# Where the high weight tiles and the w2k buffers of a two-layer mixer kernel start in SBUF

## The chip, the cores and the metric

The kernel runs on one core of a Trainium2 chip. The metric is the device time of one execution in microseconds (us). A measurement of this kernel before the change is three executions, of which the median counts; one further execution was profiled.

## The reference

Two layers of a mixer, on 256 latent and 256 context tokens of width 2048. Each layer normalises and modulates its input, multiplies it by one wide matrix, and gives the columns to three branches, whose outputs go through an output matrix. Cut to what matters here:

```python
for l in range(DEPTH):                     # 2 layers
    h = rmsnorm(x, g_pre[l]) * (1.0 + scale[:, None]) + shift[:, None]
    h_c = rmsnorm(ctx, g_pre[l]) * (1.0 + scale_c) + shift_c
    proj, proj_c = h @ w_in[l], h_c @ w_in[l]          # (256, 2048) @ (2048, 5120)
    k_ctx, v_ctx = heads(pc[4], 2), heads(pc[5], 2)    # of proj_c
    y = mixer_branches(proj, latent_attn, ...)         # gMLP, windowed attention, Fourier
    x_new = x + gate[:, None] * rmsnorm(y @ w_out[l], g_post[l])
    if not last:                                       # the context stream, in layer 0 alone
        y_c = mixer_branches(proj_c, ctx_attn, ...)
        ctx = ctx + gate_c * rmsnorm(y_c @ w_out[l], g_post[l])
    x = x_new
```

All inputs and the output are float32. In the last layer the context is needed for keys and values only.

## The kernel before

**Split operands.** TensorE multiplies in the type float32r, which keeps fewer bits than float32. So each operand is split into a high part (a cast on ScalarE) and a low part (the rest, a subtraction on VectorE), and a product is made of three matmuls: high by high, high by low, low by high. `mm3` (L576 to L578) issues them. Weights are stationary (they are loaded with LDWEIGHTS), activations are the moving operand, 512 columns wide in layer 0 (256 latent and 256 context tokens).

**Layer 1's units.** In layer 1 only the latent tokens are needed for most columns. There `hh[k]` holds the high part of the activations in its first 256 columns and the low part in the other 256, and `mm2` (L732, L733) makes the same three products with two matmuls: the high weights against all 512 columns, and the low weights against the first 256. I call the two a pair. `tunit1` runs a unit (128 output columns) as 16 pairs, one for each of 16 tiles of the inner dimension; the two units for the keys run the pairs for latent and context both. The phases of layer 1, in order, are named au, cx, ag, cg, k, v, q, bg.

```python
    def mm2(ps, w, h, k):
        PE.matmul(ps, w[0], h, start=k == 0, stop=False)
        PE.matmul(ps[:, 0:S], w[1], h[:, 0:S], start=False, stop=k == KT - 1)
```

**The stream of weights.** `Stream` (object `W`) holds all weight tiles of 128 x 1024 in the order of their use: layer 0's units, layer 0's output matrix, layer 1's units, layer 1's output matrix. Each is loaded by a DMA from SyncE's queue into one of three `raw` buffers, and `emitting` (L544, L546) casts it into a `whi` tile on ScalarE and writes the rest into a `wlo` tile on VectorE. `twins` (L554) does the same for the value weights in another arrangement. `whi` and `wlo` are rings of four buffers each. The stream runs three tiles ahead of its use (`AHEAD`). Some tiles have places of their own (`place`). A unit takes two tiles, eight of the sixteen inner tiles from each, 512 bytes of each partition for one LDWEIGHTS.

**The ring's order.** The 214 high tiles that go through the ring take the four buffers in turn, except that the tiles numbered 5, 8, 11, 14, 113, 116, 119 and 122 (from 0) take the buffer that is second in turn, since its last reader comes first there.

**Other work on the engines.** The attention, Fourier and gating branches are generators that `Later` steps between the matmuls of the units, by an estimate of the time that has passed. Their temporaries are the seven `w2k` buffers of 512 floats: queries as stationary operand, probabilities and transposed probabilities (L593, L594, L1176) as moving operand, and so on. Next to it, VectorE forms the modulation of the next layer from streamed weights (`mods`). TensorE's order is the order of the source; VectorE's, ScalarE's and SyncE's follow priorities after layer 0's first stage.

**Where tiles stand.** `HOMES` (L93) lists the tiles with long-lived places; they are allocated one behind the other, from byte 16,512 of each partition on, in steps of 32 bytes. Because the sizes ahead of them add up so, `w2k` (from 51,712), `wlo`, the activations `hh` and `hl`, and all four `whi` buffers (94,720, 98,816, 102,912, 107,008) start at multiples of 512 bytes. The small tiles (`es`, `mx`, `nm`, `den`, `rs_a`, the modulation vectors) stand behind the homes.

Of the kernel before, what the change touches and what calls it, by code (L numbers as in the profile page):

```python
# [7 lines left out]
F32 = mybir.dt.float32  # L8
F32R = mybir.dt.float32r
# [4 lines left out]
P = 128  # L14
D = 2048
KT = D // P
S = 256
# [49 lines left out]
def trunk_kernel(ctx: ExitStack, tc: tile.TileContext, xT, xhalf, cT, wss, wsl, wmod, win, wout0, wout1, const, vec, rows,  # L67
                 wmat, bs, sink, out):
    nc = tc.nc
    V, A, G, PE, DMA = nc.vector, nc.scalar, nc.gpsimd, nc.tensor, nc.sync  # L70
# [3 lines left out]
    W2K = 7  # L74
    cnt = [0]

    def sb(shape, dt, tag, bufs=1):
        cnt[0] += 1
        return pool.tile(shape, dt, tag=tag, bufs=bufs, name=f"{tag}_{cnt[0]}")

    def w2k(shape, dt=F32):
        return sb(shape, dt, "w2k", W2K)
# [5 lines left out]
    def ms_ps(name="ms"):  # L88
        cnt[0] += 1
        return psum.tile([P, 512], F32, tag="ms", bufs=2, name=f"ps_{name}_{cnt[0]}")  # L90


    HOMES = ([("ct", 32, 1), ("cs", 32, 1), ("gs0", 32, 1)] + [(f"yy{i}", 1024, 1) for i in range(8)]  # L93
             + [("join", 256, 2), ("w2k", 512, W2K), ("mraw", 1024, 2)]
             + [(tag, 1024, n) for tag, n in (("macc", 1), ("vv", 1), ("raw", 3), ("whi", 4), ("wlo", 4), ("mg", 1), ("mgl", 1))]
             + [(f"{tag}{i}", 512, 1) for i in range(KT) for tag in ("hh", "hl")]
             + [(tag, 512, 1) for tag in ("acc", "ctrh", "ctrl", "nstrh", "nstrl", "ws", "bsb", "kt1")]
             + [("identr", P, 1), ("ones", P, 1), ("red", P, 2), ("m0r", P, 1), ("rbs", S, 2), ("kt0", 2 + KT * 32, 1)])
    for tag, n, bufs in HOMES:
        sb([P, n], F32, tag, bufs)  # L100

# [9 lines left out]
    ct = sb([P, KT, 2], F32, "ct")  # L111
    vecs = sb([P, 2, NVEC], F32, "vecs")
    cst = sb([P, NKEEP - P], F32, "cst")
    ones = sb([P, P], F32, "ones")
    V.memset(ones, 1.0)
    mhalf8 = sb([P, 8], F32, "mhalf")
    mhalf = mhalf8[:, 0:4]
# [19 lines left out]
    class low:  # L137


        def __init__(self, n):  # L140
            self.n = n
# [16 lines left out]
    identr = sb([P, P], F32R, "identr")  # L158
# [5 lines left out]
    gg0 = sb([P, KT, 2], F32, "gg0")  # L164
# [223 lines left out]
    state = {"ctx": [], "phase": "", "owed": 0.0}  # L388
# [43 lines left out]
    class Later:  # L432
# [19 lines left out]
        def flush(self):  # L452
# [6 lines left out]

    OUT = list(range(8, KT)) + list(range(8))  # L460
    NHI, NLO, NRAW = 4, 4, 3
    TAIL = [(("hl0 hl1", 1), ("hl2 hl3", 1)), (("hl4 hl5", 1), ("hl6 hl7", 1)),
            (("mraw", 2), ("mraw", 2)), (("macc", 1), ("ws bsb", 1)),
            (("yy4", 1), ("yy5", 1)), (("yy6", 1), ("yy7", 1))]
# [6 lines left out]
    class Stream:  # L471
        AHEAD = 3

        def __init__(self):
            self.src, self.out, self.pos, self.stop = [], [], 0, 0
            self.raws, self.rest = [], []
            self.place, self.behind, self.twin = {}, {}, set()
            for l in range(2):
                def half(name, i, h):
                    return win[l, UIDX[name][i], h]  # L480
                for i in range(2):
                    a = [half("av", 2 * i, 0), half("au01", i, 0), half("av", 2 * i, 1),
                         half("av", 2 * i + 1, 0), half("au01", i, 1), half("av", 2 * i + 1, 1)]
                    if l == 0:
                        a.insert(3 - i, half("au2", 0, i))
                        self.place[len(self.src) + 3 - i] = AU2[i]
                    self.src += a
                for i, u in enumerate(UNITS):
                    if u[0] not in ("av", "au01") + ("au2",) * (l == 0):
                        if u[0] == "v":  # L490
                            self.twin.update((len(self.src), len(self.src) + 1))
                        self.src += [win[l, i, 0], win[l, i, 1]]
                if l == 0:
                    self.src += [wout0[j, i] for j in OUT for i in range(2)]
                else:
                    self.src += [wout1[c, i] for c in range(4) for i in range(8)]
                if l == 0:
                    n = len(self.src) - 2 * HELD
                    self.place[n] = (("mraw", 2), ("mraw", 2))
                    self.place[n + 1] = (("macc", 1), ("mg", 1))  # L500
            for i, tags in enumerate(TAIL):
                self.place[len(self.src) - len(TAIL) + i] = tags
            self.raw_place = {len(self.src) - len(TAILRAW) + i: tags for i, tags in enumerate(TAILRAW)}
# [16 lines left out]
        def load_rest(self):  # L520
            n, r = self.rest.pop(0)
            DMA.dma_start(r[:, 512:], self.src[n][:, 512:])

        def emitting(self, cut=1024):

            if len(self.raws) == len(self.out):
                self.load()
            n = len(self.out)
            r = self.raws[n]
            if n in self.twin:  # L530
                yield from self.twins(r)
                return
            tags = self.place.get(n, (("whi", NHI), ("wlo", NLO)))
            hi, lo = ([sb([P, 1024 // len(t[0].split())], F32R, tag, t[1]) for tag in t[0].split()] for t in tags)
            self.out.append((hi, lo))
            cut = min(cut, 1024 // max(len(hi), len(lo), len(r) if isinstance(r, list) else 1))
            for i in range(0, 1024, cut):
                c = slice(i, i + cut)
                ph, pl = part((hi, lo), c)
                rc, _ = part((r, r), c)  # L540
                with ExitStack() as after:
                    for i in self.behind.get(n, ()):
                        after.enter_context(tc.issue_after(i.ins))
                    A.copy(ph, rc)  # L544
                yield
                self.last = V.tensor_tensor(out=pl, in0=rc, in1=ph.bitcast(F32), op=ALU.subtract)  # L546
                yield

        def twins(self, r):

            self.out.append([sb([P, 2, 2, 256], F32R, tag, n) for tag, n in (("whi", NHI), ("wlo", NLO))])
            for i, t in enumerate(self.out[-1]):
                rc = r[:, i * 512:(i + 1) * 512].rearrange("p (k c) -> p k c", c=256)
                A.copy(t[:, :, 0], rc)  # L554
                yield
                self.last = V.tensor_tensor(out=t[:, :, 1], in0=rc, in1=t[:, :, 0].bitcast(F32), op=ALU.subtract)
                yield
# [22 lines left out]
    def part(w, c):  # L580

        def of(t):
            if not isinstance(t, list):
                return t[:, c]
            n = t[0].shape[-1]
            return t[c.start // n][:, c.start % n:c.start % n + c.stop - c.start]

        return of(w[0]), of(w[1])
# [724 lines left out]
    def finish():  # L1313
# [16 lines left out]
        later.add(turn(), YT)  # L1330
        state["phase"] = "out1"
        state["ones"] = sb([P, P], F32R, "join", 2)
        A.copy(state["ones"], ones)
        sums = sb([P, 2, 4], F32, "sums")
        gy = {}
        tot = sb([P, 2], F32, "tot")
# [65 lines left out]
    rbs = {}  # L1402
# [89 lines left out]
    with tc.manual_schedule(engines={EN.PE}):  # L1492
# [5 lines left out]
        raw = w2k([P, NFIRST])  # L1498
# [5 lines left out]
        for i in range(KT):  # L1504
# [12 lines left out]
            for a in range(2):  # L1517
                k = 2 * j + a
# [14 lines left out]
        for h, ps in enumerate((ms_ps("rs"), mm_ps("rs"))):  # L1533
            for j in range(2):
                c = slice(h * S + j * P, h * S + (j + 1) * P)
# [31 lines left out]
        state["acc"] = out_proj()  # L1567
        layer(1)
        finish()


# [75 lines left out]
```

## Time and profile before

| | |
|---|---|
| median of three executions | 1119.2 us (1117.8 to 1120.15) |
| the profiled execution | 1119.12 us |
| its span, first to last instruction | 1117.3 us |
| TensorE matmuls, busy | 1107.5 us (99%) |
| weight loads (PEld), busy | 927.7 us (83%) |
| VectorE, busy | 926.3 us (83%) |
| ScalarE, busy | 550.4 us (49%) |
| granted TensorE clock | 1.00 |

A page of the profile gives the busy time of each engine and groups of instructions; the longer answers of the trace list groups of a stretch of time (source line, engine, operation, output and input tiles, shape and type, count, then busy us, mean ns of one, and the idle time ahead of them with what ended it), or single instructions in the order of time (start in us from the span's start, duration in us, engine, line, operation). Busy time of matmuls says little: they are pipelined, each takes longer than the distance to the next, and their ends are modelled. The distance from one start to the next is what a matmul costs.

Roughly, layer 0's first stage lasts until 128 us, its units until 495 us, its output matrix until about 718 us; layer 1's first stage lasts from 729 to 763 us, its units until 1016.6 us, and its output matrix until the end.

### The profile page before, as it was taken

To read this page: it belongs to the slowest core of one execution; us is meant where nothing else is said; L and a number is where in the kernel's file an instruction comes from. 1 tells how busy PE (TensorE), PEld (TensorE's weight loads), DVE (VectorE), ACT (ScalarE), POOL (GpSimd) and SP (SyncE) were. 2 spreads that over 40 slices of the span, in tenths; PEclk is the share of its full clock that TensorE was granted. 3 is DMA by queue.
4 is the path that set the end of the run, shared out by engine and by line. 5 is a ranking of instruction groups with operands and counts; after the bars stand their busy time and mean duration, and the time that the engine had idled before them with its cause. 6 is when DMAs were issued, how large, how long until landed. Compare 5 with 4: busy or idle time off the path is not lost. (4 is left out here: it accounts for less than half of the span.)

```text
span 1117.3 us, 17365 instructions
## 1 busy us (share of the span) xinstructions
PE 1107.5 (99%) x6450; PEld 927.7 (83%) x6453; DVE 926.3 (83%) x1616; ACT 550.4 (49%) x1049; POOL 33.4 (3%) x43
## 2 busy tenths in 40 slices
PE   8999999999999999999999999999999999999998
PEld 4777888888888888888888888988888888888886
DVE  3677599999988897988988989396989789878874
ACT  4455823322235666622533324266665379867552
POOL 1000000000000000000000000030500000000000
PEclk9999999999999999999999999999999999999999
DMA  9999664566655343465556665385956686465981
GB/s 377 414 413 409 220 202 159 190 220 225 196 190 180 99 157 114 147 201 174 166 191 206 216 217 188 94 202 193 235 168 203 214 289 194 160 181 195 306 261 75
DMA packets 75525, 235.89 MB, mean 211 GB/s; under 512 B 8480, under 2 KB 15024, under 8 KB 75440
## 3 DMA queue, kind: packets, MB, share of 16 engines
q1 hardware_dynamic: 71088, 230.31, 61.5%
q0 software_dynamic: 4064, 3.69, 2.2%
q8 instruction: 50, 0.82, 0.3%
q10 hardware_dynamic: 288, 0.79, 0.2%
q14 instruction: 35, 0.29, 0.1%
HBM read 232.65 MB, written 2.10 MB: 210 GB/s over the span
## 5 line engine op out<-in xcount | busy, mean ns | idle before, releaser
L544 ACT CAST whi<-raw 128x1024 fp32r<-128x1024 f32 (+1 forms) x210 | 216.7, 1035 | 305.8 <-PE ps_t L577 203.7
L576 PE MATMUL ps_t<-hh,whi 128*128 128x512 f32 (+1 forms) x752 | 290.5, 386 | 0.0
L577 PE MATMUL ps_t<-hl,whi 128*128 128x512 f32 (+1 forms) x752 | 289.7, 385 | 0.0
L578 PE MATMUL ps_t<-hh,wlo 128*128 128x512 f32 (+1 forms) x752 | 289.6, 385 | 0.0
L546 DVE TENSOR_TENSOR wlo<-raw,whi 128x1024 fp32r<-128x1024 f32 (+1 forms) x210 | 250.9, 1198 | 43.2 <-ACT whi L544 38.7
L319 DVE SCALAR_TENSOR_TENSOR macc<-mraw,cs,macc 128x512 f32<-128x512 f32 x360 | 251.1, 744 | 13.4 <-DMA mraw<-in_wmod_dram 12.8
L732 PE MATMUL ps_t<-hh,whi 128*128 128x512 f32 x512 | 184.4, 399 | 0.0
L578 PEld LDWEIGHTS ps_t<-hh,wlo 128*128 128x128 f32 x752 | 141.3, 188 | 28.7
L576 PEld LDWEIGHTS ps_t<-hh,whi 128*128 128x128 f32 x752 | 141.4, 188 | 27.0
L577 PEld LDWEIGHTS ps_t<-hl,whi 128*128 128x128 f32 x752 | 141.4, 188 | 26.2
L733 PE MATMUL ps_t<-hh,wlo 128*128 128x256 f32 x512 | 143.0, 279 | 0.0
L732 PEld LDWEIGHTS ps_t<-hh,whi 128*128 128x128 f32 x512 | 96.3, 188 | 21.2
L733 PEld LDWEIGHTS ps_t<-hh,wlo 128*128 128x128 f32 x512 | 96.6, 189 | 0.4
L576 PE MATMUL ps_y<-whi,hh 128*128 128x512 f32 x104 | 41.3, 397 | 0.0
L578 PE MATMUL ps_y<-whi,hh 128*128 128x512 f32 x104 | 40.6, 390 | 0.0
L577 PE MATMUL ps_y<-wlo,hh 128*128 128x512 f32 x104 | 40.5, 390 | 0.0
L593 ACT CAST w2k<-ps_tp 128x512 fp32r<-128x512 f32 x40 | 23.3, 584 | 21.3 <-PE ps_scc L577 13.7
L594 DVE TENSOR_TENSOR w2k<-ps_tp,w2k 128x512 fp32r<-128x512 f32 x40 | 27.4, 684 | 3.7 <-ACT w2k L593 2.4
L606 POOL TENSOR_TENSOR rs_b<-rs_a,mhalf 128x2 f32<-128x2 f32 (+1 forms) x7 | 6.3, 897 | 753.0 <-DVE mx L1422 583.1
L1156 ACT ACTIVATE w2k<-w2k,den 128x512 f32<-128x512 f32 (+1 forms) x48 | 28.2, 646 | 0.7 <-DVE den L1151 0.6
L811 PE MATMUL ps_av<-whi,hh 128*128 128x512 f32 x64 | 24.3, 395 | 0.2 <-ACT hh L681 0.2
L576 PE MATMUL ps_o<-w2k,vv 128*128 128x256 f32 x80 | 24.5, 306 | 0.0
(493 smaller groups left out, 1820.6 us busy)
## 6 DMA issues: line engine op xcount, KB each, us to landing
raw<-in_win_dram SPq DMA_DIRECT2D x158, 512.0 KB, 4.3
mraw<-in_wmod_dram SPq DMA_DIRECT2D x128, 512.0 KB, 4.4
raw<-in_wout_dram SPq DMA_DIRECT2D x60, 512.0 KB, 4.5
mraw<-in_wsl_dram SPq DMA_DIRECT2D x12, 512.0 KB, 7.2
yy<-in_xhalf_dram SPq DMA_DIRECT2D x7, 512.0 KB, 7.4
mg<-in_wsl_dram SPq DMA_DIRECT2D x7, 512.0 KB, 8.7
mgl<-in_wsl_dram SPq DMA_DIRECT2D x7, 512.0 KB, 9.2
yy<-in_xhalf_dram POOLq DMA_DIRECT2D x28, 128.0 KB, 7.6
```

What stands on the lines that cost most here:

```text
L319: V.scalar_tensor_tensor(out=acc[:, s], in0=w[:, kk % 2], scalar=c, in1=acc[:, s], op0=ALU.mult, op1=ALU.add)
L544: A.copy(ph, rc)
L546: self.last = V.tensor_tensor(out=pl, in0=rc, in1=ph.bitcast(F32), op=ALU.subtract)
L576: PE.matmul(ps, st[0], mv[0], start=start, stop=False)
L577: PE.matmul(ps, st[0], mv[1], start=False, stop=False)
L578: PE.matmul(ps, st[1], mv[0], start=False, stop=stop)
L593: A.copy(hi, src)
L594: V.tensor_tensor(out=lo, in0=src, in1=hi.bitcast(F32), op=ALU.subtract)
L732: PE.matmul(ps, w[0], h, start=k == 0, stop=False)
L733: PE.matmul(ps[:, 0:S], w[1], h[:, 0:S], start=False, stop=k == KT - 1)
L811: PE.matmul(ps, st[a], mv[b], start=start and (a, b) == (0, 0), stop=stop and (a, b) == (1, 0))
L1156: A.activation(prob[i][:, b * w:(b + 1) * w], prob[i][:, b * w:(b + 1) * w], AF.Copy, scale=den[:, c:c + 1])
```

## The change

- The ring `whi` becomes four tiles `whi0` to `whi3` of 1024 + 16 floats. A method `high` hands them out; its list `OVERTAKEN` holds the numbers at which the second in turn is taken.
- A high tile normally begins 16 floats (64 bytes) behind the start of its tile, which is a multiple of 256 bytes. For the two tiles of each unit of layer 1 that runs in pairs (all but `av`, `au01` and `v`), it begins at the tile's start, 64 bytes lower.
- So that these starts come out, each `whi` tile has 192 bytes of small tiles ahead of it: a modulation vector of 32 floats, and two buffers of four floats. Each such group takes 4352 bytes. The tiles start at 191,168 for the first group; the normal places of the four high tiles are 191,232, 195,584, 199,936 and 204,288.
- `w2k` comes behind them, 64 bytes after a multiple of 256 (208,448), and `kt0` behind `w2k` (222,784). All homes that stood behind `w2k` move down by 14,336 bytes or, behind the `whi` ring, by 30,720.
- `ones` shrinks from 128 to 32 columns; the one reader of all 128 broadcasts a column instead.

```diff
+    ASIDE = 16
     HOMES = ([("ct", 32, 1), ("cs", 32, 1), ("gs0", 32, 1)] + [(f"yy{i}", 1024, 1) for i in range(8)]
-             + [("join", 256, 2), ("w2k", 512, W2K), ("mraw", 1024, 2)]
-             + [(tag, 1024, n) for tag, n in (("macc", 1), ("vv", 1), ("raw", 3), ("whi", 4), ("wlo", 4), ("mg", 1), ("mgl", 1))]
+             + [("join", 256, 2), ("mraw", 1024, 2)]
+             + [(tag, 1024, n) for tag, n in (("macc", 1), ("vv", 1), ("raw", 3), ("wlo", 4), ("mg", 1), ("mgl", 1))]
              + [(f"{tag}{i}", 512, 1) for i in range(KT) for tag in ("hh", "hl")]
              + [(tag, 512, 1) for tag in ("acc", "ctrh", "ctrl", "nstrh", "nstrl", "ws", "bsb", "kt1")]
-             + [("identr", P, 1), ("ones", P, 1), ("red", P, 2), ("m0r", P, 1), ("rbs", S, 2), ("kt0", 2 + KT * 32, 1)])
+             + [("identr", P, 1), ("red", P, 2), ("m0r", P, 1), ("rbs", S, 2)])
+    for i, (tag, small) in enumerate((("gs1", "es"), ("sh0", "mx"), ("sh1", "nm"), ("gg0", "den"))):
+        HOMES += [(tag, 32, 1), (small, 4, 2), (f"whi{i}", 1024 + ASIDE, 1)]
+    HOMES += [("rs_a", 4, 2), ("w2k", 512, W2K), ("kt0", 2 + KT * 32, 1)]
...
-    ones = sb([P, P], F32, "ones")
+    ones = sb([P, 32], F32, "ones")
...
+    OVERTAKEN = 5, 8, 11, 14, 113, 116, 119, 122
...
+            self.highs = list(range(NHI))
...
                         if u[0] == "v":
                             self.twin.update((len(self.src), len(self.src) + 1))
+                        elif l:
+                            self.aside.update((len(self.src), len(self.src) + 1))
...
+        def high(self, aside=False):
+            i = self.highs.pop(1 if self.nhi in OVERTAKEN else 0)
+            self.highs.append(i)
+            self.nhi += 1
+            o = 0 if aside else ASIDE
+            return sb([P, 1024 + ASIDE], F32R, f"whi{i}")[:, o:o + 1024]
...
-            tags = self.place.get(n, (("whi", NHI), ("wlo", NLO)))
-            hi, lo = ([sb([P, 1024 // len(t[0].split())], F32R, tag, t[1]) for tag in t[0].split()] for t in tags)
+            tags = self.place.get(n, (None, ("wlo", NLO)))
+            hi, lo = ([sb([P, 1024 // len(t[0].split())], F32R, tag, t[1]) for tag in t[0].split()] if t
+                      else [self.high(n in self.aside)] for t in tags)
...
-            self.out.append([sb([P, 2, 2, 256], F32R, tag, n) for tag, n in (("whi", NHI), ("wlo", NLO))])
+            self.out.append([t.rearrange("p (k a c) -> p k a c", k=2, a=2) for t in (self.high(), sb([P, 1024], F32R, "wlo", NLO))])
...
-        A.copy(state["ones"], ones)
+        A.copy(state["ones"], ones[:, 0:1].to_broadcast([P, P]))
```

More of the change, by code (lines that the diff above doesn't have):

```diff
@@ L476, in __init__ @@
             self.raws, self.rest = [], []
-            self.place, self.behind, self.twin = {}, {}, set()
+            self.place, self.behind, self.twin, self.aside, self.nhi = {}, {}, set(), set(), 0
+            self.highs = list(range(NHI))
             for l in range(2):
```

## The prediction

> **What bounds the kernel now.** I read the page's first part, then the busy times by stage, then the matmuls one by one in the order of time.
>
> ```profile
> PE 1107.5 (99%) x6450; PEld 927.7 (83%) x6453; DVE 926.3 (83%) x1616; ACT 550.4 (49%) x1049; POOL 33.4 (3%) x43
> ...
> L576 PE MATMUL ps_t<-hh,whi 128*128 128x512 f32 (+1 forms) x752 | 290.5, 386 | 0.0
> ```
> ```profile
> 345.00:495.00 150.00, 150.00 (x804) 127.46 (x804) 130.45 (x243) 92.38 (x203) 0.00 (x0) 1.00 0.45 138
> 908.00:993.00 85.00, 85.00 (x520) 75.36 (x519) 75.12 (x152) 71.93 (x149) 0.00 (x0) 1.00 0.57 182
> ```
>
> The rows by stage give the stretch, its length, then the busy time and count of PE, PEld, DVE, ACT and POOL, and the granted clock. TensorE is busy for 1107.5 of 1117.3 us, and in the attention stages of both layers it has no hole at all, at a granted clock of 1.00. So nothing that another engine does shows in the time unless TensorE begins to wait; what counts is how far apart its matmuls start. The ends of matmuls are modelled, so I use starts. First the matmuls of one width in a row, in layer 0 (512 columns, then 256):
>
> ```profile
> 559.87 0.39 PE L576 MATMUL ps_t<-hh,whi 128*128 128x512 f32 x1
> ...
> 561.23 0.39 PE L576 MATMUL ps_t<-hh,whi 128*128 128x512 f32 x1
> ```
> ```profile
> 713.74 0.28 PE L577 MATMUL ps_t<-hl,whi 128*128 128x256 f32 x1
> ...
> 714.94 0.28 PE L578 MATMUL ps_t<-hh,wlo 128*128 128x256 f32 x1
> ```
>
> Six matmuls of 512 columns take 1.36 us, 227 ns each; ten of 256 take 1.20 us, 120 ns each. The 256 columns between the two cost 107 ns, 0.417 ns a column, so each matmul has some 13 ns (227 - 512 x 0.417) beside its columns. Now layer 1's pairs, in which a 512-column matmul (L732) and a 256-column one (L733) alternate, at two places:
>
> ```profile
> 846.91 0.39 PE L732 MATMUL ps_t<-hh,whi 128*128 128x512 f32 x1
> ...
> 849.68 0.39 PE L732 MATMUL ps_t<-hh,whi 128*128 128x512 f32 x1
> ```
> ```profile
> 1011.20 0.40 PE L732 MATMUL ps_t<-hh,whi 128*128 128x512 f32 x1
> ...
> 1012.26 0.40 PE L732 MATMUL ps_t<-hh,whi 128*128 128x512 f32 x1
> ...
> 1013.32 0.40 PE L732 MATMUL ps_t<-hh,whi 128*128 128x512 f32 x1
> ```
>
> At the first place eight pairs take 2.77 us, 346 ns a pair, which is just 227 + 120. At the second three pairs take 1.06 us, twice over: 353 ns a pair. It is the same work from tiles at the same distances, so the pairs have at least two rhythms, and the worse one costs 7 ns a pair. The reader should see how the next weights are fetched meanwhile:
>
> ```profile
> 1013.32 0.40 PE L732 MATMUL ps_t<-hh,whi 128*128 128x512 f32 x1
> 1013.33 0.19 PEld L733 LDWEIGHTS ps_t<-hh,wlo 128*128 128x128 f32 x1
> ```
>
> Each weight load starts within 0.01 us of the matmul that it runs beside. Two streams read the SBUF together; in this kernel every fp32r operand of the pairs starts at a multiple of 512 bytes. The change puts one of the two, the load of the high weights, at another distance from the other. That is the only way that I see from the diff to the time.
>
> **The change part by part.** The profiled execution took 1119.12 us (1117.3 of span and 1.8 outside); the median of the three runs is 1119.2, so I work from 1119.12 and add nothing.
>
> *The high weights of layer 1's units, 64 bytes lower.* 32 units have 16 or, for the two k units, 32 pairs: 544 pairs. What they lose now:
>
> ```profile
> L732 PE MATMUL ps_t<-hh,whi 128*128 128x512 f32 x512 | 184.4, 399 | 0.0
> L733 PE MATMUL ps_t<-hh,wlo 128*128 128x256 f32 x511 | 142.7, 279 | 0.0
> ...
> L1176 PE MATMUL ps_tp<-identr,w2k 128*128 128x128 f32 x64 | 9.6, 272 | 0.0
> ```
> ```profile
> L732 PE MATMUL ps_t<-hh,whi 128*128 128x512 f32 x81 | 28.1, 394 | 0.0
> L733 PE MATMUL ps_t<-hh,wlo 128*128 128x256 f32 x81 | 22.4, 277 | 0.0
> ```
> ```profile
> 940.39 0.48 PE L732 MATMUL ps_t<-hh,whi 128*128 128x512 f32 x1
> 940.70 0.28 PE L733 MATMUL ps_t<-hh,wlo 128*128 128x256 f32 x1
> ```
>
> The first group is from 763 to 1016.6 us, the second from the undisturbed stretch from 824.6 to 852.4. The means differ by 5 and 2 ns, 7 ns a pair, 3.6 us over 512. Part of that is no rhythm: a pair behind four transposes begins with a matmul of 0.48 us instead of 0.40. The 64 transposes are 16 groups, of which half precede a pair, and about as many pairs follow the other small matmuls: 16 x 0.08 = 1.3 us, which stays. That leaves 2.3 us. The other way round: the 256 pairs of the q and bg units run mostly in the worse rhythm, 256 x 7 ns = 1.8 us. I take 2.0 us as what there is to win if all pairs fall into the better rhythm. No row shows a load at a distance of 64 bytes, so the price of one pair is bounded from the nearest rows: at best the load of the high weights costs its neighbour nothing, and the 13 ns beside the columns go, 544 x 13 = 7.1 us; at worst all 544 pairs run like the slow rhythm, 7 ns for the 288 or so that do not yet, 2.0 us more. Between them I take the better rhythm for all, -2.0 us, because the row of the undisturbed stretch is the nearest one and because a rhythm that depends on how two streams meet is what a new distance would break.
>
> On this the Trainium skill has a rule against the change: "SBUF — State Buffer", section "Who interferes with whom", gives TensorE two independent read ports, one for the moving operand and one for the weight load, and says that it never waits on anyone. By it the sum of this part would be nothing. The trace does not agree that nothing is waited for: the pairs differ by 7 ns on equal work at a clock of 1.00, though it cannot say whether addresses are why.
>
> *The buffers of w2k 64 bytes on.* They are the operands of the attention's matmuls, and so of what disturbs the rhythm. In layer 0's attention (345 to 495 us) against its quiet part (500 to 640 us):
>
> ```profile
> L577 PE MATMUL ps_t<-hl,whi 128*128 128x512 f32 x154 | 60.2, 391 | 0.0
> L576 PE MATMUL ps_t<-hh,whi 128*128 128x512 f32 x153 | 60.2, 393 | 0.0
> L578 PE MATMUL ps_t<-hh,wlo 128*128 128x512 f32 x153 | 59.8, 391 | 0.0
> ```
> ```profile
> L578 PE MATMUL ps_t<-hh,wlo 128*128 128x512 f32 x207 | 80.5, 389 | 0.0
> L576 PE MATMUL ps_t<-hh,whi 128*128 128x512 f32 x206 | 80.1, 389 | 0.0
> ```
>
> The three means are 4, 2 and 2 ns up, 8 ns a group of three, 1.2 us over 153 groups. How much of that comes from where w2k stands no row tells: from all of it gained (1.2) to as much again lost. I take half, -0.6 us.
>
> *The ring in four tiles.* The pop list repeats the order in which the ring of four handed out its 214 tiles, so each cast waits for the same readers as before. The waits of the cast, its length and that of the subtraction, from 763 to 1016.6 us:
>
> ```profile
> ACT whi L544 <- PE ps_t L732: 22.3, 21, 2.4
> ```
> ```profile
> L546 DVE TENSOR_TENSOR wlo<-raw,whi 128x1024 fp32r<-128x1024 f32 x65 | 79.4, 1221 | 16.5 <-ACT whi L544 14.7 <-PE ps_v L1235 1.4
> ```
>
> ScalarE waits for TensorE to free a tile, up to 2.4 us at a time; it runs ahead. Were the order wrong, a cast would wait for a later reader, and it is this lead that would be used up first; behind it on ScalarE stand the attention's copies, and TensorE waits for the subtraction. I price it at nothing.
>
> *VectorE and ScalarE on shifted tiles.* One row has an operand off 256 bytes already: the sine table in cst, 104 bytes behind a multiple.
>
> ```profile
> L1106 DVE TENSOR_TENSOR mgl<-mgl,cst x20: 415/417/428, 300.7 to 966.6; 128x256 f32<-128x256 f32 x20
> ```
> ```profile
> L739 DVE TENSOR_TENSOR join<-join,ps_t 128x256 f32<-128x256 f32 x33 | 13.6, 411 | 3.1 <-ACT join L738 3.1
> ```
>
> 417 ns against 411 for the same size on aligned tiles: nothing to speak of, and hidden, since TensorE is the one that is full. If each of the 64 subtractions cost 6 ns more it would be 0.4 us of VectorE, in stages where it has 10 of 85 us free.
>
> *Ones with 32 columns.* The memset and the copy that are touched:
>
> ```profile
> L115 DVE MEMSET ones<- x1: 165/165/165, 0.8 to 0.8; 128x128 f32 x1
> L1333 ACT CAST join<-ones x1: 302/302/302, 1019.0 to 1019.0; 128x128 fp32r<-128x128 f32 x1
> ```
>
> The first is in the start, the second gets a broadcast source; its reader comes microseconds later. Nothing.
>
> **The sum:** 1119.1 - 2.0 - 0.6 = 1116.5 us.
>
> **The rivals.** *Addresses do not matter* (for it: within the pairs the two rhythms occur at equal distances, so something other than the address chooses between them, and the skill's rule stands on this side). Then only layout changes and the time stays 1119.1. Against it: I know of nothing else that would make equal pairs unequal. Chance 0.29.
>
> *The load becomes free.* If the weight load and the moving operand collide because both start at multiples of 512, the distance of 64 bytes frees the pair of more than the bad rhythm, up to 7.1 us beyond it: 1109.4, and at half of that 1113.0, which I take as this case's time. For it: 13 ns beside the columns of every matmul. Against it: the 13 ns are the same for 512 and 256 columns and may be no collision. Chance 0.10.
>
> *Layer 0 loses its rhythm,* which ends slower. Before, all four high tiles start at multiples of 512. With 64 + 1024 + 16 floats and their small neighbours each takes 4352 bytes, 17 x 256, so that two of the four stand at odd multiples of 256, for all of layer 0 too. Of 752 groups of three at L576 all but 32 are 512 wide; half of the 720 take their weights from these two tiles. If those groups run like the ones in the attention stage, 8 ns each, that is 360 x 8 = 2.9 us, and with nothing won in layer 1 the time is 1122.0. It decides from 2.2 us, 6 ns a group, and has to eat up the 2.6 of the forecast first if that comes true. For it: the quiet stretch at 389 without exception has only distances of 512 multiples. Against it: within those, 512 more or less makes no difference. Chance 0.16.
>
> **How the numbers follow.** The forecast has 0.45, the rivals 0.29, 0.10 and 0.16. A measurement of this kernel tells about 0.2% (2.2 us) from no change. The forecast's own range is a gain of 0.8 to 4.5 us (1118.3 to 1114.6); its point lies just past the bound, and I put 0.10 of its 0.45 below it. Faster: 0.35 + 0.10 = 0.45; same: 0.29 + 0.10 = 0.39; slower 0.16. The range goes from 1111.5, within the case of the free load, to 1121.5, short of the full loss in layer 0; outside it I leave about 0.15.
>
> **What would show it.** Right: in layer 1 the L732 and L733 rows fall from 399 and 279 towards 394 and 277, eight pairs take 2.77 us late in the bg units as well, and ps_t in layer 0's attention falls from 393 and 391 towards 389, while PE stays free of holes. The free load would show as pairs below 340 ns. Layer 0's loss would show between 500 and 640 us, where every row is at 389 now. Wrong would be pairs that still take 353 ns, or a new rhythm above it; or idle time of PE in front of L732 that ends with a cast or a subtraction, which would mean the order of the tiles does matter.

## The result, and the profile after

The changed kernel takes 1115.74 us (median of ten executions, 1115.26 to 1116.89) against 1118.82 us for the kernel before (ten, 1117.8 to 1120.15): a ratio of 0.9972, with a 95% interval of 0.9963 to 0.9981. The profiled execution took 1115.65 us, with a span of 1113.9 us; before it was 1119.12 and 1117.3.

Lines below `high` are numbered 16 higher: the pair is L748 and L749 (before L732 and L733), `mm3` is L592 to L594, the cast L560, the subtraction L562. The page's first part:

```profile
PE 1104.0 (99%) x6450; PEld 926.4 (83%) x6453; DVE 926.4 (83%) x1616; ACT 550.7 (49%) x1049; POOL 33.4 (3%) x43
```

It is the same work, of which only PE became shorter, by 3.5 us. The loads (PEld) lie beside matmuls, so their 1.3 us less count for nothing. By stage, the attention stages of layer 0 and of layer 1:

```profile
345.00:495.00 150.00, 150.00 (x806) 127.45 (x805) 130.72 (x243) 92.34 (x203) 0.00 (x0) 1.00 0.44 139
905.00:990.00 85.00, 84.86 (x525) 75.42 (x524) 75.77 (x154) 72.99 (x150) 0.00 (x0) 1.00 0.61 186
```

Layer 0 gets through 806 matmuls where it got through 804, layer 1 through 525 where it got through 520, at the same clock. TensorE is still full but for 0.14 us. The pairs of layer 1 (763 to 1013.2 us), and below them the row of before for the third:

```profile
L748 PE MATMUL ps_t<-hh,whi 128*128 128x512 f32 x512 | 181.2, 394 | 0.0
L749 PE MATMUL ps_t<-hh,wlo 128*128 128x256 f32 x511 | 141.9, 278 | 0.0
L748 PE MATMUL ps_t<-hl,whi 128*128 128x512 f32 x32 | 12.4, 389 | 0.0
```
```profile
L732 PE MATMUL ps_t<-hl,whi 128*128 128x512 f32 x32 | 12.6, 395 | 0.0
```

The means fall from 399 and 279 to 394 and 278. Each matmul's end is modelled, so the starts count. Two places in the order of time:

```profile
897.38 0.40 PE L748 MATMUL ps_t<-hh,whi 128*128 128x512 f32 x1
...
900.18 0.40 PE L748 MATMUL ps_t<-hh,whi 128*128 128x512 f32 x1
...
1002.43 0.39 PE L748 MATMUL ps_t<-hh,whi 128*128 128x512 f32 x1
...
1005.15 0.39 PE L748 MATMUL ps_t<-hh,whi 128*128 128x512 f32 x1
```

At each place eight pairs lie between the two rows. Late in the bg units they take 2.72 us, 340 ns a pair (353 before). At 897 us they take 2.80 us, 350 ns a pair (347 before). Neither 340 nor 350 was a steady rhythm before. Over all pairs that another pair follows directly, from start to start:

| stretch (us) | before, ns | after, ns |
|---|---|---|
| 763 to 800 | 349.7 | 347.8 |
| 800 to 823 | 351.9 | 341.3 |
| 823 to 876 | 346.7 | 340.1 |
| 876 to 908 | 346.5 | 350.0 |
| 908 to 990 | 353.2 | 344.7 |
| from 990 | 353.3 | 340.2 |
| all 477 | 350.1 | 343.3 |

Of the 477, 316 now take 339 to 341 ns, and 121 take 348 to 351. All matmuls come in the same order as before, so each can be compared with itself: 0.29 us of lead have come together by 729 us (all layer 0), 0.51 by 763, 2.3 by 874; between there and 908 us 0.5 is given back; it is 2.7 at 993 and 3.5 at 1016.6 us, where the units end. The output matrix adds nothing (3.45 at 1098 us). So 3.0 of the 3.45 us come in layer 1's units. Most of the 0.22 between 729 and 763 us are no matter of the moved weights: in that stretch the kernel before has one wait of TensorE for a split tile, which the changed kernel has not:

```profile
PE ps_av L577 <- DVE wlo L546: 0.2, 1, 0.2
```

Layer 0, whose weights stand at multiples of 256 now, in its attention (345 to 495 us):

```profile
L592 PE MATMUL ps_t<-hh,whi 128*128 128x512 f32 x154 | 60.6, 394 | 0.0
L594 PE MATMUL ps_t<-hh,wlo 128*128 128x512 f32 x154 | 60.3, 392 | 0.0
L593 PE MATMUL ps_t<-hl,whi 128*128 128x512 f32 x154 | 60.0, 389 | 0.0
```

394, 392 and 389 against 393, 391 and 391 is the same sum of 1175. From start to start a group of three that another follows directly went from 689.6 to 688.9 ns. In the quiet stretch (500 to 640 us) a group takes 680.0 ns in both kernels, with every row at 389.

### The profile page after: what moved, and what is told of

It reads as the page before. It is cut to its first block, busy times and chain, and to the rows that moved or that the text cites. A ratio compares the mean times of both kernels' runs of the same rounds, so it can differ in the third digit from the quotient of the medians.

```text
span 1113.9 us, 17364 instructions
## 1 busy us (share of the span) xinstructions
PE 1104.0 (99%) x6450; PEld 926.4 (83%) x6453; DVE 926.4 (83%) x1616; ACT 550.7 (49%) x1049; POOL 33.4 (3%) x43
## 5 line engine op out<-in xcount | busy, mean ns | idle before, releaser
L560 ACT CAST whi<-raw 128x1024 fp32r<-128x1024 f32 (+1 forms) x210 | 216.6, 1035 | 302.3 <-PE ps_t L593 186.0
L592 PE MATMUL ps_t<-hh,whi 128*128 128x512 f32 (+1 forms) x752 | 290.9, 387 | 0.0
L594 PE MATMUL ps_t<-hh,wlo 128*128 128x512 f32 (+1 forms) x752 | 289.8, 385 | 0.0
L562 DVE TENSOR_TENSOR wlo<-raw,whi 128x1024 fp32r<-128x1024 f32 (+1 forms) x210 | 251.0, 1199 | 40.6 <-ACT whi L560 34.7
L748 PE MATMUL ps_t<-hh,whi 128*128 128x512 f32 x512 | 181.2, 394 | 0.0
L594 PEld LDWEIGHTS ps_t<-hh,wlo 128*128 128x128 f32 x752 | 141.3, 188 | 28.7
L592 PEld LDWEIGHTS ps_t<-hh,whi 128*128 128x128 f32 x752 | 141.4, 188 | 26.5
L749 PE MATMUL ps_t<-hh,wlo 128*128 128x256 f32 x512 | 142.2, 278 | 0.0
L748 PEld LDWEIGHTS ps_t<-hh,whi 128*128 128x128 f32 x512 | 96.2, 188 | 19.3
L749 PEld LDWEIGHTS ps_t<-hh,wlo 128*128 128x128 f32 x512 | 96.2, 188 | 0.4
L592 PE MATMUL ps_y<-whi,hh 128*128 128x512 f32 x104 | 41.3, 397 | 0.0
L594 PE MATMUL ps_y<-whi,hh 128*128 128x512 f32 x104 | 40.6, 391 | 0.0
L592 PE MATMUL ps_o<-w2k,vv 128*128 128x256 f32 x80 | 24.4, 305 | 0.0
```

What stands on the lines that cost most here:

```text
L592: PE.matmul(ps, st[0], mv[0], start=start, stop=False)
L594: PE.matmul(ps, st[1], mv[0], start=False, stop=stop)
```

## The experiments

The theory to begin with (A): the distance in bytes between the stationary and the moving operand sets how far a pair is slowed. The rivals: what else moves (`w2k`, the ring's four tiles) does it, or any new place would do as well (B). In the diffs a tile's normal place is `o = ASIDE`, a multiple of 256. Medians are us; the kernel before, run beside each, had 1118.8 to 1119.0.

**One half each.** `w2k_only` leaves the pairs at multiples of 256:

```diff
-            o = 0 if aside else ASIDE
+            o = ASIDE
```

> The layout of the changed kernel, but every high tile at its multiple of 256, layer 1's pairs too; only w2k and kt0 stand 64 bytes on. Theory A (the distance between the high weights and the moving operand sets what a pair costs): no pair in a row at 340 ns, pairs at 346 to 353 as before, time within 1.0 us of before. Theory B (any new place that breaks the slow rhythm does it, w2k included): pairs at 340 ns appear here too, and 1 to 2.5 us of the 3.1 us are gained.

`whi_only` keeps the pairs 64 bytes lower and puts `w2k` back on a multiple of 256:

```diff
-    HOMES += [("rs_a", 4, 2), ("w2k", 512, W2K), ("kt0", 2 + KT * 32, 1)]
+    HOMES += [("w2k", 512, W2K), ("kt0", 2 + KT * 32, 1), ("rs_a", 4, 2)]
```

> The changed kernel with w2k and kt0 at multiples of 256, the high tiles of layer 1's pairs 64 bytes lower. Theory A: long rows of pairs at 340 ns, 2.3 to 3.5 us faster than before. Theory B: without the moved w2k the attention still throws the pairs into the slow rhythm, at most 1.5 us faster than before, with 353 ns a pair from 993 us on.

Measured: 1118.11, a ratio of 0.9993 (0.9984 to 1.0002), and 1115.67, 0.9970 (0.9960 to 0.9981). The groups of layer 1, first `w2k_only`, then `whi_only`:

```profile
L748 PE MATMUL ps_t<-hh,whi 128*128 128x512 f32 x512 | 184.4, 399 | 0.0
L749 PE MATMUL ps_t<-hh,wlo 128*128 128x256 f32 x511 | 142.7, 279 | 0.0
```
```profile
L748 PE MATMUL ps_t<-hh,whi 128*128 128x512 f32 x512 | 180.8, 393 | 0.0
L749 PE MATMUL ps_t<-hh,wlo 128*128 128x256 f32 x511 | 141.7, 277 | 0.0
```

With the pairs at the old distance the rows are those of before, to the digit, though the high tiles stand in new places. With only the pairs moved the whole gain is there. `w2k` brings nothing that can be told from none: layer 0's groups of three in the attention take 689.6 ns before, 689.0 in `w2k_only`, 689.3 in `whi_only` and 688.9 with both.

**The other direction.** `whi_up` puts each tile ahead of its small neighbours and the pairs 64 bytes higher:

```diff
-        HOMES += [(tag, 32, 1), (small, 4, 2), (f"whi{i}", 1024 + ASIDE, 1)]
+        HOMES += [(f"whi{i}", 1024 + ASIDE, 1), (tag, 32, 1), (small, 4, 2)]
...
-            o = 0 if aside else ASIDE
+            o = ASIDE if aside else 0
```

> The changed kernel with the high tiles of layer 1's pairs 64 bytes higher instead of lower than a multiple of 256. Theory A with a distance that counts in both directions: pairs at 340 ns as in the changed kernel, 2.5 to 3.5 us faster than before. Theory A with a direction (the load must read behind the moving stream): pairs at 346 ns or above, within 1 us of before or slower. Theory B: about as fast as the changed kernel, since any new place does.

Measured 1118.26, 0.9994 (0.9985 to 1.0002). Eight pairs:

```profile
841.04 0.40 PE L748 MATMUL ps_t<-hh,whi 128*128 128x512 f32 x1
...
843.84 0.40 PE L748 MATMUL ps_t<-hh,whi 128*128 128x512 f32 x1
```

They take 2.80 us, 350 ns, and do so from 763 us to the end of the units: 349.9 over all. So it matters where the high weights stand, and to which side; merely leaving the multiple of 256 is worth nothing.

**Other distances.** Three kernels change only the offset of the pairs: `o = 12`, `8` or `4 if aside else ASIDE` for 16, 32 and 48 bytes lower. For 80 and 96, `ASIDE = 24` (the small neighbours take 32 bytes less ahead of a tile that is 32 bytes longer), with `o = 4` and `o = 0`.

> The changed kernel with the high tiles of layer 1's pairs 16 bytes lower than a multiple of 256 instead of 64. If the price of a load falls in proportion to the distance: rows of pairs near 345 ns, a quarter of the way from 346.7 to 340, about 1 us faster than before. If it goes in whole steps of 64 bytes: pairs at 346 to 353 ns as before the change, within 1 us of before.

> The changed kernel with the high tiles of layer 1's pairs 32 bytes lower instead of 64. In proportion: rows of pairs near 343 ns, 1.5 to 2.5 us faster than before. In steps of 64 bytes: as before the change. If any lower place is enough: 340 ns.

> The changed kernel with the high tiles of layer 1's pairs 48 bytes lower instead of 64. So far the steady pair took 346.7 or 353.3 ns at 0 bytes, 350 at 16, 345 to 347 at 32, 340 or 350 at 64, 349 at 96. If 64 is one end of a slope that falls from 16 on: 341 to 344 ns, about 2.5 us faster than before. If 64 is a point of its own: 346 ns or more, at most 1.5 us faster than before.

> The changed kernel with the high tiles of layer 1's pairs 80 bytes lower instead of 64. If the price has its low at 64 and rises evenly on both sides: 343 to 346 ns, 1.5 to 2.5 us faster than before. If 64 is a point of its own: 349 to 350 ns as at 96 bytes, within 1 us of before. If the low lies between 64 and 96: below 340 ns and faster than the changed kernel.

> The changed kernel with the high tiles of layer 1's pairs 96 bytes lower instead of 64. In proportion: below 340 ns, near 337, 1 us or more faster than the changed kernel. In steps of 64 bytes: 340 ns, as in the changed kernel. If 64 bytes are the best place and the price rises again behind it: 343 ns or more.

| pairs lower by | median | ratio | a pair, all | its rhythms |
|---|---|---|---|---|
| -64 (higher) | 1118.26 | 0.9994 | 349.9 | 350 |
| 0 | 1118.11 | 0.9993 | 350.0 | 346.7, 353.3 |
| 16 | 1118.29 | 0.9995 (0.9985 to 1.0004) | 349.3 | 350 |
| 32 | 1117.31 | 0.9985 (0.9976 to 0.9995) | 346.6 | 344.6 to 347, 353.3 |
| 48 | 1116.83 | 0.9982 (0.9973 to 0.9992) | 346.9 | 346.7 |
| 64 | 1115.74 | 0.9972 (0.9963 to 0.9981) | 343.3 | 340, 350 |
| 80 | 1117.78 | 0.9990 (0.9980 to 0.9999) | 349.6 | 346.7, 353.3 |
| 96 | 1118.03 | 0.9995 (0.9985 to 1.0004) | 349.4 | 349.3 |

Eight pairs 48 bytes lower and eight 96 lower:

```profile
840.96 0.39 PE L748 MATMUL ps_t<-hh,whi 128*128 128x512 f32 x1
...
843.74 0.39 PE L748 MATMUL ps_t<-hh,whi 128*128 128x512 f32 x1
```
```profile
841.27 0.39 PE L749 MATMUL ps_t<-hh,whi 128*128 128x512 f32 x1
...
844.06 0.39 PE L749 MATMUL ps_t<-hh,whi 128*128 128x512 f32 x1
```

2.78 and 2.79 us, against 2.72 at 64. The time is smallest at 64. From 16 to 64 the medians fall step by step, and at 32 and 48 the intervals lie below 1, so it is no case of one odd distance against all others. It does not go in proportion either: 16 bytes gave 349.3 and not 345 ns, and 48 no shorter pair than 32. On the far side no slope is seen: 80 and 96 bytes have 349.6 and 349.4 ns, and their intervals overlap.

**All high weights lower.** `whi_all` takes layer 0 and the output matrices along:

```diff
-            o = 0 if aside else ASIDE
+            o = 0
```

> The changed kernel with every high tile 64 bytes lower, layer 0's units and the first stages too. Theory A taken to its end (each load of high weights costs 6.7 ns less): two of three matmuls of layer 0's groups load high weights, the quiet group of three falls from 680 to about 667 ns, some 9 us faster than the changed kernel. Rival C (matmuls of one width in a row keep 13 ns beside their columns wherever the weights stand): the quiet group stays at 680 ns, within 1.5 us of the changed kernel.

Measured 1121.80, 1.0024 (1.0015 to 1.0034). The pairs keep their 343.4 ns. Layer 0's quiet stretch (500 to 640 us) and layer 1's output matrix (1018 to 1098 us), then the output matrix of the changed kernel (1018 to 1094 us):

```profile
L592 PE MATMUL ps_t<-hh,whi 128*128 128x512 f32 x204 | 80.2, 393 | 0.0
L594 PE MATMUL ps_t<-hh,wlo 128*128 128x512 f32 x205 | 80.0, 390 | 0.0
```
```profile
L592 PE MATMUL ps_y<-whi,hh 128*128 128x512 f32 x101 | 40.8, 404 | 0.0
L593 PE MATMUL ps_y<-wlo,hh 128*128 128x512 f32 x101 | 40.1, 397 | 0.0
```
```profile
L592 PE MATMUL ps_y<-whi,hh 128*128 128x512 f32 x97 | 38.6, 398 | 0.0
L593 PE MATMUL ps_y<-wlo,hh 128*128 128x512 f32 x97 | 37.8, 390 | 0.0
```

A quiet group of three goes from 680.0 to 686.7 ns, where the expectations had 667 or still 680. A group of the output matrix that another follows directly goes from 689.6 to 707.5 ns. In that matrix of layer 1 the roles are changed (L1355): the activations are stationary and the weights are the moving operand, which these rows name first. So there it was the moving tile that stood 64 bytes lower. At 729 us this kernel is 3.85 us behind the one before, at 1016.7 only 0.8, at 1098 again 2.8. The 64 bytes that help a pair harm matmuls of equal width, whichever of the two operands has them.

**Low weights lower.** `wlo_low` puts the ring `wlo` behind 192 bytes of small tiles, 64 bytes below a multiple of 256, with all high weights at multiples; `both_low` has the pairs' high weights lower as well. The activations behind the ring move by 256 bytes in both. The main part of the edit:

```diff
-             + [(tag, 1024, n) for tag, n in (("macc", 1), ("vv", 1), ("raw", 3), ("wlo", 4), ("mg", 1), ("mgl", 1))]
+             + [(tag, 1024, n) for tag, n in (("macc", 1), ("vv", 1), ("raw", 3))]
+             + [("gs1", 32, 1), ("es", 4, 2), ("wlo", 1024, 4), ("mx", 4, 2), ("mg", 1024, 1), ("mgl", 1024, 1)]
...
```

> All high tiles at multiples of 256 as before the change, and all low tiles 64 bytes lower, in both layers. If each load that stands 64 bytes lower costs the pair 6.7 ns less whichever of the two matmuls it runs beside: pairs at 340 ns in layer 1. If only the load beside the 256-column matmul counts (the high weights'): pairs at 346 ns or above. In layer 0 a group of three has one such load, half of what it had with all high tiles lower: 683 ns instead of 680 in the quiet part, 2 us slower there.

> The changed kernel with all low tiles, of both layers, 64 bytes lower too. Layer 0 as with the low tiles alone: quiet groups of three at 693 ns, about 7 us lost there. In layer 1, if the two loads of a pair have prices of their own: 340 ns plus what the low tiles alone cost (2 ns or more), so 342 or above. If what counts is that the two loads of a pair stand alike: back to 346 ns or above. If both gain: 333 ns.

Measured 1126.80, 1.0074 (1.0059 to 1.0089), and 1128.91, 1.0092 (1.0075 to 1.0108). The quiet stretch of `wlo_low`:

```profile
L596 PE MATMUL ps_t<-hh,wlo 128*128 128x512 f32 x202 | 79.8, 395 | 0.0
L595 PE MATMUL ps_t<-hl,whi 128*128 128x512 f32 x202 | 79.5, 394 | 0.0
L594 PE MATMUL ps_t<-hh,whi 128*128 128x512 f32 x203 | 79.3, 391 | 0.0
```

All three rows are up from 389, to 693.3 ns a group, where 683 was expected, and `wlo_low` is 7.7 us behind by 729 us. Eight pairs of layer 1 in `wlo_low`, then in `both_low`:

```profile
840.53 0.39 PE L750 MATMUL ps_t<-hh,whi 128*128 128x512 f32 x1
...
843.33 0.39 PE L750 MATMUL ps_t<-hh,whi 128*128 128x512 f32 x1
```
```profile
840.61 0.40 PE L750 MATMUL ps_t<-hh,whi 128*128 128x512 f32 x1
...
843.44 0.39 PE L750 MATMUL ps_t<-hh,whi 128*128 128x512 f32 x1
```

They take 2.80 and 2.83 us. Over all, the pairs of `wlo_low` have 348.9 ns, against 350.0 with no weights lower. In `both_low`, where both weights of a pair stand 64 bytes lower, they have 351.7, and the gain is gone. So it takes one of the two at 64 bytes, the high one.

**The ring without its list.** `in_turn` hands the four tiles out strictly in turn:

```diff
-    OVERTAKEN = 5, 8, 11, 14, 113, 116, 119, 122
+    OVERTAKEN = ()
```

> The changed kernel with an empty list of overtaken tiles: the four high tiles are taken strictly in turn. If the lead of ScalarE covers it: idle time of TensorE as in the changed kernel and the same time within 1 us. If the list is needed: casts that wait for a later reader at the tiles 5 to 14 (layer 0's first stage) and 113 to 122 (around the boundary between the layers), TensorE idle there in front of matmuls that wait for the subtraction, 1 to 10 us slower than the changed kernel. The pairs of layer 1 keep their 340 and 350 ns either way.

Measured 1119.64, 1.0003 (0.9994 to 1.0012): the whole gain is gone, though the pairs have their 343.1 ns. Against the changed kernel 0.2 us are lost until 729 us, and 3.8 in layer 1's first stage. That stage by 2 us in `in_turn`, then by 10 us in the changed kernel (columns as above; the last two are the share and the GB/s of DMA):

```profile
751.00:753.00 2.00, 0.51 (x1) 0.19 (x1) 1.30 (x2) 2.00 (x7) 0.00 (x0) 1.00 0.04 5
753.00:755.00 2.00, 1.63 (x4) 1.34 (x5) 2.00 (x4) 1.58 (x3) 0.00 (x0) 0.52 0.23 43
755.00:757.00 2.00, 2.00 (x9) 1.62 (x7) 2.00 (x4) 0.00 (x0) 0.00 (x0) 0.62 0.97 350
757.00:759.00 2.00, 2.00 (x11) 1.69 (x10) 1.18 (x4) 0.00 (x0) 0.00 (x0) 1.00 0.93 301
```
```profile
745.00:755.00 10.00, 10.00 (x50) 8.35 (x49) 9.76 (x20) 5.96 (x11) 0.87 (x1) 1.00 0.87 244
755.00:765.00 10.00, 10.00 (x51) 8.22 (x50) 4.28 (x5) 6.41 (x8) 0.00 (x0) 1.00 0.55 207
```

What PE waited for in `in_turn` between 729 and 765 us:

```profile
PE ps_av L593 <- DVE wlo L562: 1.7, 1, 1.7
PE ps_av L592 <- ACT whi L560: 0.3, 1, 0.3
```

TensorE stands idle for 2.0 us in front of split tiles, in two parts with one matmul between them, and then the granted clock falls to about half for two stretches of 2 us, which costs 2 x (0.48 + 0.38) = 1.7 us more: 3.7 of the 3.8. The changed kernel has neither. The cast before this hole:

```profile
749.12 2.00 ACT L560 CAST whi<-raw 128x1024 fp32r<-128x1024 f32 x2 [1.56 <-DMA raw<-in_win_dram]
```

That the casts came late because a tile was still being read, and the loads behind them as well, is what the order suggests; the trace shows only that this cast waited 1.6 us for its DMA.

## Why the prediction was right or wrong

*Addresses at all: right.* The kernel with `w2k` moved and the changed one differ by nothing but 64 bytes in the pairs' high weights, and take 1118.11 and 1115.74 us. So the rival that addresses do not matter fell. The rule of the Trainium skill that stood on its side ("SBUF — State Buffer", section "Who interferes with whom": two independent read ports, TensorE waits on nobody) does not give this kernel's time: with nothing else moved, the mean pair took 350.0 or 343.3 ns. Whether it is reads that wait, or something inside TensorE that depends on the address, no run here tells; nor whether the distance to the moving tile counts or the place of the weights alone, since the moving tiles of the pairs stood at multiples of 256 in every run.

*High weights lower, -2.0 us: sign and place right, size and rhythm wrong.* The step that failed is "all pairs fall into the better rhythm" of 346 ns. They fell into two new ones: two thirds into 340 ns, a quarter into 350. These 121 had 349.3 ns on average before, so they won nothing, and the 36 of them from 876 to 908 us, which had 346.7, lost. The term, summed over the pairs from start to start, measured -3.6 us: -2.5 in the steps behind L748, -0.8 behind L749, -0.3 in the 32 pairs of `hl`. The v units, whose high weights stand at multiples of 256 in both kernels, gave 0.4 back. The -2.0 was a fair price for what it priced, though its 7 ns a pair came from mean durations: from start to start the pairs of before averaged 350.1 ns, and all at 346.7 would have brought 544 x 3.4 ns = 1.9 us. What it left out is a rhythm better than any in the profile of before. That a pair behind transposes keeps its long first matmul came true (0.48 us at 938.2 us). The rows fell to 394 and 278 as forecast, but as the mean of 340 and 350.

*The free load: not this either.* The prediction read 346 ns as "just 227 + 120". The single steps say otherwise. Over the undisturbed pairs from 823 to 876 us the step behind the 512-column matmul is 231.6 ns on average and the step behind the 256-column one 115.0; in the changed kernel they are 227.0 and 113.0. So two thirds of what a pair won came out of the step behind the 512-column matmul. The 768 columns of a pair are 320 ns at the prediction's 0.417 ns, so what stands beside them fell from some 27 to 20 ns, an estimate. That is half of the 13 ns that this rival gave away, and its sign, pairs below 340 ns, did not come: the steady ones stay at 340.0. The measured 1115.7 us lies nearer to the forecast's 1116.5 than to this rival's 1113.0. Which of a pair's two loads the 7 ns belong to, the steps do not tell.

*w2k, -0.6 us: not seen.* Layer 0's groups in the attention lost 0.7 of 689.6 ns, 0.1 us over 154, and the sum of their three rows stayed at 1175; all of layer 0 gained 0.29 us. With the pairs lower, the medians without and with `w2k` moved are 1115.67 and 1115.74; with the pairs at multiples of 256 and `w2k` moved it was 1118.11, with an interval that holds no change. So the excess of these groups over 680 ns is much the same with `w2k` at a multiple of 256 and 64 bytes behind one.

*The ring in four tiles, at nothing: right.* ScalarE's longest wait for a tile is still 2.4 us in layer 1, and TensorE has no wait for it:

```profile
ACT whi L560 <- PE ps_t L748: 19.4, 20, 2.4
```
```profile
L562 DVE TENSOR_TENSOR wlo<-raw,whi 128x1024 fp32r<-128x1024 f32 x65 | 79.4, 1222 | 16.0 <-ACT whi L560 12.9 <-PE ps_v L1251 2.0 <-PE ps_t L749 0.5
```

The lead that was said to be used up first is indeed used up without the list, but at a place that the prediction did not name, layer 1's first stage, and the hole costs nearly twice its length through the clock. *VectorE on shifted tiles, at nothing: right*, 1222 ns against 1221.

*Layer 0 loses its rhythm: fell.* Its quiet groups stay at 680.0 ns although two of four tiles stand at odd multiples of 256. The danger was real at another distance: at 64 bytes they lose 6.7 (high weights) or 13.3 ns (low weights). I had looked at the multiples of 256, where nothing happens.

The sum came out 0.8 us low in gain (1116.5 against 1115.7). The pair term was 1.6 too small, the `w2k` term up to 0.6 too large, and the 0.4 that the v units lost and the 0.2 of the wait in layer 1's first stage were not in it. That these partly cancel is luck.

What stays open: why 64 bytes, why a pair settles at 340 in one place and at 350 in another, and whether moving the activations of the pairs by 64 bytes does the same, which was not tried. By an estimate the quarter of the pairs at 350 is some 1.4 us (544 / 4 x 10 ns) that a steady 340 would still bring; no run had it, and none was measurably faster than the changed kernel.

## What to carry to other kernels

Where TensorE has no holes, compare the distance from start to start of equal matmuls: more than one value means time that no wait shows, and where the load's tile starts against the moving tile may set it. Try such a distance stage by stage: the 64 bytes that gave 3 us here cost 4 to 8 us where they were given to layer 0. When a ring is taken apart into tiles, its order is part of the kernel, and one hole of 2 us, with the clock that it costs, can take as much as the change brings.

## What the runs showed of the hardware

The pairs of matmuls with weight loads settled into repeating rhythms (340, 346.7, 350, 353.3 ns) that last for up to 50 us; where the rhythm changes, other matmuls stand between the pairs. The place of the high weights alone moved the mean pair from 350.0 to 343.3 ns at a clock of 1.00, and 16 bytes more or less (48 or 64 lower) from 346.9 to 343.3. Groups of three matmuls of 512 columns took 680.0 ns with all weights at multiples of 256, 686.7 with the high ones 64 bytes lower and 693.3 with the low ones. A hole of 2.0 us in a TensorE that was full otherwise was followed by a mean granted clock of 0.52 and 0.62 in the next two stretches of 2 us, that is by half clock for 2 x (0.48 + 0.38) / 0.5 = 3.4 us. The Trainium skill, "TensorE: Matmul & The Clock Gate", section "What's actually happening", has two clock states, full and half, set by the activity in windows of some 3.4 us, and puts the half clock behind an idle window of that length. The half clock and its length agree, but here 2.0 us of idle time were enough.
